# Batch-normalised matmul on one Trainium2 core: the first chunk of the last column tile in two halves

## The chip, the core and the metric

The kernel runs on one core of one Trainium2 chip. The metric is the device time of one execution in microseconds (us), lower is better. Four runs of the kernel before the change gave 218.57, 218.74, 219.96 and 220.45 us; their median is 219.35 us. One of them, the one of 218.57 us, was also profiled. The profiled execution has a span of 216.7 us from its first to its last instruction, so 1.87 us of its time lie outside the span.

## What is computed

```python
batch, m, k, n = 16, 512, 1024, 768

def reference(x, weight, gamma, beta, eps):
    y = np.matmul(x, weight)
    mean = np.mean(y, axis=(0, 1), keepdims=True)
    var = np.var(y, axis=(0, 1), keepdims=True)
    y_norm = (y - mean) / np.sqrt(var + eps)
    return (gamma * y_norm + beta).astype(np.float32)
```

All 8192 rows of `x` go through one 1024 x 768 matrix. Each of the 768 columns is then normalised with its own mean and variance over all 8192 rows. So no output of a column can be written before the last row of that column has been multiplied.

## The kernel before

**Tiling.** The 8192 rows are cut into C = 16 chunks of CH = 512, and each chunk into RT = 4 row tiles of 128. A chunk also has QPC = 2 halves of QR = 256 rows. The 768 columns are cut into NT = 6 tiles of 128. Column tiles 0, 1 and 2 go mostly by another way (rows on the partitions, with sums built up during the load); tiles 3, 4 and 5 are made with columns on the partitions: the 128 columns of the tile lie on 128 partitions and the 512 rows of a chunk lie along the free axis (`mm`, line 189). Statistics are then taken along the free axis with `bn` (line 311), and the product is kept in bf16 in SBUF with `keep` (line 342). The buffer that holds it is `y(nt, c)` (line 299), a slice of a tile that three chunks share.

**How a column tile is written out.** When all 16 chunks of a column tile have their statistics, VectorE (DVE) and ScalarE (ACT) work out one scale and one shift for each column: `finish` (line 361) for the last tile. Then each chunk goes through four steps, on four engines:

1. `norm` (line 375): DVE or ACT multiplies and adds, in place, on 128 x 512 bf16.
2. `turn_y` (line 387) lines up one transpose for each row tile; `turn_one` (line 396) issues it on TensorE (PE). Columns are on partitions and rows have to be there for the output, so each 128 x 128 block is transposed into PSUM (`o_ps`).
3. `out_copy` (line 400): ACT copies PSUM to an SBUF buffer and widens to float32.
4. `store` (line 415): SyncE (SP) issues the transfer to `out`. Each row of the output gets 128 floats, so the pieces written are 512 bytes long.

Column tiles 3 and 4 take chunks in pairs (512 KB for each store, from a buffer named `ring`). The last pair of column tile 4 is held back (`HELD = 1`) and issued by `held_outputs` (line 549) in the gap in which the last statistics are worked out. The last column tile, number 5, takes single chunks (256 KB for each store) in `last_outputs` (line 558). Its float32 buffers come from the pool of 11 buffers (`xtpool`, bufs = C - EARLY) that held the transposed input; they are called `o_sb`.

**What sets the order.** Nothing is issued where it is written. `at(t, fn, ...)` appends an event with a planned time; at the end all events are sorted by that time and called in turn. `seq` chains each instruction to the one before it on its engine, so the sorted list is the order of every engine. The planned times only set the order; at run time an engine runs its instructions in order and waits where an input or a buffer isn't ready. For the last chunk of the last column tile the matmul, its statistics and its copy are already split in two (`mm_half`, `bn_half`, `keep_half`, lines 325 to 340). Pools hand out buffers in turn: PSUM has 8 for the tag `b`, which the accumulators and the transposes share.

The order of the work at the end is therefore: on ACT the copy of the held pair (`ring`), the second `keep_half`, then 16 copies `o_sb`; on DVE `finish`, then 16 times `norm`; on PE the 8 transposes of the held pair, then 64 transposes; on SP the store of the held pair, then 16 stores.

Of the kernel before, what the change touches and what calls it, by code (L numbers as in the profile page):

```python
# [10 lines left out]
def kernel(  # L11
# [23 lines left out]
    nc = tc.nc  # L35
# [3 lines left out]
    ALU = mybir.AluOpType  # L39
# [9 lines left out]
    RT = CH // P  # L49
    C = M // CH  # L50
    QR = 256
    QPC = CH // QR
# [24 lines left out]
    def seq(bi):  # L77

        ins = bi.ins
        prev = last.get(ins.engine)  # L80
        if prev is not None:
            tc.add_manual_dep(
                ins, prev,
                mybir.DependencyInfo(mybir.DependencyClass.NoSync, mybir.DependencyReason.DATA),
                reason="order",
            )
        last[ins.engine] = ins.name
        return bi
# [6 lines left out]
    scale = singles.tile([P, NT], f32)  # L95
    shift = singles.tile([P, NT], f32)
# [202 lines left out]
    def y(nt, c):  # L299
        key, i = ((nt, c // GY), c % GY) if nt >= GA else ((0, c), nt)  # L300
        if key not in ygrp:
            y_sb = ypool.tile([P, GY, CH], bf16, tag="y")
            ygrp[key] = y_sb
        return ygrp[key][:, i]
# [70 lines left out]
    def norm(nt, c, eng):  # L375
# [5 lines left out]
        else:  # L381
# [2 lines left out]
                op0=ALU.mult, op1=ALU.add,  # L384
            ))

    def turn_y(nts, m0, tiles):

        o_ps = psum.tile([P, tiles, len(nts), P], bf16, tag="b")
        ops[nts, m0] = o_ps  # L390
        for s in range(tiles):
            c, i = divmod(m0 // P + s, RT)
            for a, nt in enumerate(nts):
                turns.append(((nts, m0), o_ps[:, s, a], y(nt, c)[:, i * P:(i + 1) * P]))
# [30 lines left out]
    def at(t, fn, *args):  # L425
        events.append((t, len(events), fn, args))
# [93 lines left out]
    for c in range(C):  # L520
        if c in COLS:
            for nt in range(GA):
                if c:
                    at(tk - 3.4 + 0.8 * nt, norm, nt, c, "act")
            for s in range(0, RT, 2):
                at(tk + 0.7 * s, turn_y, ga, c * CH + s * P, 2)
                at(tk + 0.7 * s + 1.9, out_copy, ga, c * CH + s * P, "act")
                at(tk + 0.7 * s + 2.7, store, ga, c * CH + s * P, 2)
            tk += 9.6 if c else 7.2
        else:  # L530
            for s in range(0, RT, 2):
                at(tr, norm_rows, c, s)
                at(tr + 1.1, shift_rows, c, s)
                at(tr + 3.0, store_rows, c, s)
                tr += 1.85

    def outputs(nt, t0, step):
        for b in range(C // 2):
            tb = t0 + step * b
            if nt == NT - 2 and b >= C // 2 - HELD:  # L540
                held.append(b)
                continue
            for i in range(2):
                at(tb - 2.2 + 0.5 * i, norm, nt, 2 * b + i, "act" if tb < tr + 2.0 and i == 0 else "dve")
            at(tb, turn_y, (nt,), 2 * b * CH, 2 * RT)
            at(tb + 2.2, out_copy, (nt,), 2 * b * CH, "act")
            at(tb + 2.3, store, (nt,), 2 * b * CH, 2 * RT)

    def held_outputs(nt, t0):

        for i, b in enumerate(held):
            for j in range(2):
                at(t0 - 3.0 + 0.4 * (2 * i + j), norm, nt, 2 * b + j, "dve")
            at(t0 + 0.05, turn_y, (nt,), 2 * b * CH, 2 * RT)
            at(t0 + 0.7 + 0.1 * i, out_copy, (nt,), 2 * b * CH, "act")
            at(t0 + 0.75 + 0.1 * i, store, (nt,), 2 * b * CH, 2 * RT)

    def last_outputs(nt, t0):

        for c in range(C):  # L560
            tb = t0 + 0.6 * c
            at(tb - 1.2, norm, nt, c, "dve")
            at(tb, turn_y, (nt,), c * CH, RT)
            at(tb + 0.5, out_copy, (nt,), c * CH, "act", True)
            at(tb + 0.6, store, (nt,), c * CH, RT)
# [3 lines left out]
    for nt in range(GA, NT):  # L569
        for c in range(EARLY, C):  # L570
            if (nt, c) == (NT - 1, C - 1):
                for q in range(QPC):
                    at(pe, mm_half, q)
                    pe += 0.9
                    at(pe + 0.2, bn_half, q)
                    at(pe + (0.4 if q == 0 else 1.0), keep_half, q)
                at(pe - 2.4, sum_up)
                continue
            for jws in halves:
                unit(nt, c, MM_US / 2 + (0.12 if nt == GA else 0.17), jws)  # L580
        if nt < NT - 1:
            at(pe + 0.55, finish_var, nt)
            at(pe + 1.6, finish_affine, nt)
        else:
            at(pe + 0.55, finish, nt)
        if nt == GA:
            outputs(nt, S + 37.0, 2.3)
        elif nt < NT - 1:
            outputs(nt, pe + 4.6, 1.85)
        else:  # L590
            held_outputs(nt - 1, pe)
            last_outputs(nt, pe + 3.0)
# [39 lines left out]
```

## Time and profile before

| what | us |
|---|---|
| median of four runs | 219.35 |
| lowest and highest run | 218.57, 220.45 |
| the profiled run | 218.57 |
| its span | 216.7 |
| PE busy (share of the span) | 200.3 (92%) |
| DVE busy | 155.8 (72%) |
| ACT busy | 120.8 (56%) |
| POOL busy | 134.2 (62%) |
| mean granted TensorE clock | 0.98 |

Over the whole span PE is the busiest engine. That share is an average, and the change touches only the last stage, from about 200 us on. In that stage these are the instructions of the last column tile (first and last start in us from the start of the span, and the duration of one):

| step | engine | how many | first start | last start | ns of one |
|---|---|---|---|---|---|
| `norm` | DVE | 16 | 200.16 | 205.02 | about 400 |
| transposes | PE | 64 | 200.63 | about 205.7 | about 220, one each 83 |
| `out_copy` to `o_sb` | ACT | 16 | 201.06 | 208.22 | 585 to 778 |
| issue of a store | SP | 16 | 201.67 | 211.23 | 372 to 637 |

Durations of neighbours overlap in the pipelines of the engines: DVE starts a `norm` every 0.32 us and ACT a copy every 0.48 us.

### The profile page before, as it was taken

What the parts mean: (1) busy time and instruction counts of PE and PEld (TensorE: products, weight loads), DVE (VectorE), ACT (ScalarE), POOL (GpSimd) and SP (SyncE); (2) the same over time, 40 slices, a digit from 0 to 9 for tenths busy, and PEclk for the clock granted to TensorE, in tenths of its full rate; (3) what the DMA queues carried; (4) which work ended last, traced back from release to release, by engine and by line L of the source; (5) the groups of instructions that cost most, each with busy time, mean ns of one, the idle gap of its engine ahead of it and who ended that gap; (6) DMA issues with size and microseconds to landing.
All of it is one profiled execution on the core that took longest, in us unless ns stands there. A gap on an engine that the chain in (4) does not pass through costs nothing.

```text
span 216.7 us, 3451 instructions
## 1 busy us (share of the span) xinstructions
PE 200.3 (92%) x1178; PEld 105.0 (48%) x1178; DVE 155.8 (72%) x263; ACT 120.8 (56%) x227; POOL 134.2 (62%) x153
## 2 busy tenths in 40 slices
PE   7998999999999999999999999999999979997900
PEld 2463545454544565645565544444444435554600
DVE  3223788896988789998654369978899999728900
ACT  2002463554553477646666415866866789976950
POOL 7888595978774799944558204999995963000000
PEclk9999999999999999999999999999999999999975
DMA  5999999999999999993000000897877989999998
GB/s 62 171 207 189 195 196 194 197 197 196 195 191 197 194 196 196 196 196 41 2 3 0 0 0 0 312 363 274 323 287 291 332 272 366 344 347 278 285 346 242
DMA packets 70161, 43.75 MB, mean 202 GB/s; under 512 B 4096, under 2 KB 69632, under 8 KB 70144
## 3 DMA queue, kind: packets, MB, share of 16 engines
q0 software_dynamic: 34624, 18.36, 61.8%
q1 hardware_dynamic: 35520, 25.18, 36.0%
q8 instruction: 9, 0.15, 0.3%
q14 instruction: 8, 0.07, 0.1%
HBM read 36.71 MB, written 25.17 MB: 285 GB/s over the span
## 4 chain that ended last, share of the span: by engine, by line
PE 75%; DVE 8%; DMA 5%; POOL 3%; issue 2%; ACT 2%; ACTq 1%; POOLq 0%
PE y_ps L196 39%; PE y_ps L186 29%; PE o_ps L398 5%; DMA w_sb<-in_weight_dram 2%; DMA ring<-in_x_dram 2%; DVE stats L316 2%; DVE y_sb L382 2%; DVE ring L283 2%; POOL w_sb L149 2%; DVE o_sb L283 1%; ACT o_sb L411 1%; POOL ring L162 1%; PE y_ps L330 1%; PE a_ps L272 1%; PE tot_ps L232 1%
## 5 line engine op out<-in xcount | busy, mean ns | idle before, releaser
L196 PE MATMUL y_ps<-xT_sb,w_sb 128*128 128x512 bf16 (+1 forms) x484 | 117.6, 381 | 0.7 <-DMA w_sb<-in_weight_dram 0.7
L196 PEld LDWEIGHTS <-w_sb 128*128 128x128 bf16 x484 | 46.0, 96 | 58.1 <-issue 1.6
L343 ACT CAST y_sb<-y_ps 128x512 bf16<-128x512 f32 x59 | 34.6, 587 | 52.7 <-DVE stats L316 49.8
L186 PE MATMUL y_ps<-w_sb,xT_sb 128*128 128x384 bf16 x384 | 63.4, 326 | 0.0
L162 POOL DMA_DIRECT2D ring<-in_x_dram x72 | 45.2, 633 | 12.2 <-DVE xT_sb L174 6.7
L316 DVE BATCH_NORM_STATS2 stats<-y_ps 128x6 f32<-128x512 f32 x58 | 39.1, 684 | 18.7 <-PE y_ps L196 18.7
L186 PEld LDWEIGHTS <-xT_sb 128*128 128x128 bf16 x384 | 37.6, 98 | 25.6
L174 DVE STREAM_TRANSPOSE xT_sb<-ring 128x1024 f32<-128x1024 f32 (+1 forms) x34 | 39.5, 1169 | 13.8 <-DMA ring<-in_x_dram 13.7
L212 POOL TENSOR_TENSOR sum<-sum,sq_sb 128x384 f32<-128x384 f32 x38 | 38.0, 1001 | 17.3 <-ACT sq_sb L208 15.7
L398 PE MATMUL o_ps<-ident,y_sb 128*128 128x128 bf16 x240 | 38.2, 219 | 3.6 <-DVE y_sb L382 2.5
L289 POOL TENSOR_TENSOR ring<-ring,sum 128x768 f32<-128x768 f32 x17 | 31.0, 1845 | 13.1 <-ACT sum L274 12.1
L215 DVE TENSOR_TENSOR sum<-y_ps,sum 128x384 f32<-128x384 f32 x48 | 26.1, 544 | 13.8 <-ACT sq_sb L208 12.7
L208 ACT ACTIVATE sq_sb<-y_ps 128x384 f32<-128x384 f32 x48 | 23.4, 493 | 13.9 <-PE y_ps L186 10.6
L221 ACT CAST y_sb<-y_ps 128x384 bf16<-128x384 f32 x48 | 22.9, 477 | 9.0 <-DVE sum L215 8.8
L411 ACT CAST ring<-o_ps 128x1024 f32<-128x1024 bf16 (+1 forms) x24 | 22.5, 955 | 4.3 <-PE o_ps L398 2.8
L398 PEld LDWEIGHTS <-y_sb 128*128 128x128 bf16 x240 | 19.4, 97 | 8.6 <-DVE y_sb L382 3.3
L382 DVE TENSOR_SCALAR y_sb<-y_sb,scale,shift 128x512 bf16<-128x512 bf16 x43 | 22.0, 562 | 0.0
L283 DVE TENSOR_TENSOR ring<-y_sb,a_ps 128x768 f32<-128x768 bf16 x17 | 15.8, 937 | 0.0
L289 POOL TENSOR_TENSOR o_sb<-o_sb,sum 128x768 f32<-128x768 f32 x7 | 13.1, 1868 | 2.9 <-DVE o_sb L283 2.9
L377 ACT ACTIVATE y_sb<-y_sb,shift,scale 128x512 bf16<-128x512 bf16 x17 | 13.5, 816 | 0.0
L155 PE MATMUL idle_ps<-idle_sb 128*128 128x512 bf16 x38 | 11.3, 466 | 1.2 <-DVE idle_sb L103 1.2
L411 ACT CAST o_sb<-o_ps 128x512 f32<-128x512 bf16 x16 | 7.9, 679 | 0.3 <-PE o_ps L398 0.3
(62 smaller groups left out, 50.1 us busy)
## 6 DMA issues: line engine op xcount, KB each, us to landing
ring<-in_x_dram POOLq DMA_DIRECT2D x56, 256.0 KB, 8.7
out_dram<-ring SPq DMA_DIRECT2D x25, 384.0 KB, 3.1
out_dram<-ring SPq DMA_DIRECT2D x16, 512.0 KB, 5.0
out_dram<-o_sb SPq DMA_DIRECT2D x16, 256.0 KB, 3.7
out_dram<-o_sb SPq DMA_DIRECT2D x7, 384.0 KB, 3.5
ring<-in_x_dram POOLq DMA_DIRECT2D x16, 128.0 KB, 5.1
w_sb<-in_weight_dram POOLq DMA_DIRECT2D x8, 96.0 KB, 4.5
w_sb<-in_weight_dram POOLq DMA_DIRECT2D x4, 192.0 KB, 5.0
```

The costliest lines, as they stand in the source:

```text
L162: seq(nc.gpsimd.dma_start(x_bf[32 * i:32 * i + 32], src[:, :, KQ * i:KQ * (i + 1)]))
L174: seq(nc.vector.transpose(dst[:, half, :, jw0:jw1], src[:, :, jw0:jw1]))
L186: seq(nc.tensor.matmul(y_ps, xT[c][:, jw, s * P:(s + 1) * P, e], w_sb[:, jw, e, 0:NA], start=(jw == 0 and e == 0), stop=(jw == JW - 1 and ...
L196: seq(nc.tensor.matmul(y_ps, w_sb[:, jw, e, nt * P:(nt + 1) * P], xT[c][:, jw, q0 * QR:q1 * QR, e], start=(jw == 0 and e == 0 and q0 == 0) ...
L212: seq(eng.tensor_add(acc, acc, py.pop(("sq", c, s))))
L215: seq(nc.vector.tensor_add(sum1, py["row", c, s][:, 0:NA], sum1))
L289: seq(nc.gpsimd.tensor_add(o_sb, o_sb, sum1[:, None, :].to_broadcast([P, 2, NA])))
L316: seq(nc.vector.bn_stats(stats_of(nt)[:, i, :], py[nt, c]))
L343: seq(nc.scalar.copy(y(nt, c), py.pop((nt, c))))
L382: seq((nc.vector if eng == "dve" else nc.gpsimd).tensor_scalar(y(nt, c), y(nt, c), scale[:, nt:nt + 1], shift[:, nt:nt + 1], op0=ALU.mult, ...
L398: seq(nc.tensor.transpose(dst, src, ident))
L411: seq(nc.scalar.copy(o_sb, src))
```

## The change

The first chunk (c = 0) of the last column tile is taken in two halves of 256 rows. Each half has its own `norm_half` on DVE (128 x 256 instead of 128 x 512), its own PSUM tile with two transposes, its own copy on ACT (128 x 256) into its own `o_sb`, and its own store (128 KB instead of 256 KB). Chunks 1 to 15 are as before.

```diff
+    def norm_half(nt, c, q):
+        part = y(nt, c)[:, q * QR:(q + 1) * QR]
+        seq(nc.vector.tensor_scalar(
+            part, part, scale[:, nt:nt + 1], shift[:, nt:nt + 1], op0=ALU.mult, op1=ALU.add))
+
     def turn_y(nts, m0, tiles):
...
         for c in range(C):
             tb = t0 + 0.6 * c
+            if c == 0:
+
+                for q in range(QPC):
+                    at(tb - 1.2, norm_half, nt, c, q)
+                    at(tb, turn_y, (nt,), q * QR, RT // QPC)
+                    at(tb + 0.4 + 0.1 * q, out_copy, (nt,), q * QR, "act", True)
+                    at(tb + 0.4 + 0.1 * q, store, (nt,), q * QR, RT // QPC)
+                continue
             at(tb - 1.2, norm, nt, c, "dve")
             at(tb, turn_y, (nt,), c * CH, RT)
             at(tb + 0.5, out_copy, (nt,), c * CH, "act", True)
```

In the compiled order of the engines this is one more instruction on DVE, on ACT and on SP, each at the place of the first chunk; the number and the order of the transposes on PE stay as they were, and so does everything ahead of this place.

## Prediction

> **What bounds the kernel now.** The page says PE 92% busy, but the change lies behind the last matmul, so I read the end alone. First the table of stages: busy time of each engine and, in the last two columns, the mean busy share of the DMA engines and what they moved.
>
> ```profile
> core 0: us, PE busy (x) PEld busy (x) DVE busy (x) ACT busy (x) POOL busy (x), PEclk, DMA share, GB/s
> 190.00:198.00 8.00, 8.00 (x57) 4.54 (x55) 4.29 (x10) 5.68 (x9) 0.00 (x0) 1.00 1.16 348
> 198.00:199.50 1.50, 0.97 (x13) 0.72 (x11) 0.93 (x4) 0.65 (x3) 0.00 (x0) 1.00 0.99 292
> 199.50:201.50 2.00, 0.87 (x12) 0.68 (x12) 1.79 (x8) 1.71 (x4) 0.00 (x0) 1.00 0.10 31
> 201.50:203.00 1.50, 1.50 (x22) 1.01 (x19) 1.50 (x6) 1.50 (x5) 0.00 (x0) 1.00 1.14 344
> 203.00:207.00 4.00, 2.87 (x36) 1.92 (x34) 2.41 (x8) 4.00 (x10) 0.00 (x0) 1.00 1.15 346
> 207.00:211.00 4.00, 0.00 (x0) 0.00 (x0) 0.00 (x0) 2.00 (x5) 0.00 (x0) 0.65 1.15 346
> 211.00:215.00 4.00, 0.00 (x0) 0.00 (x0) 0.00 (x0) 0.00 (x0) 0.00 (x0) 0.50 1.15 345
> 215.00:215.25 0.25, 0.00 (x0) 0.00 (x0) 0.00 (x0) 0.00 (x0) 0.00 (x0) 0.50 0.64 183
> 215.25:216.70 1.45, 0.00 (x0) 0.00 (x0) 0.00 (x0) 0.00 (x0) 0.00 (x0) 0.50 0.00 0
> ```
>
> There is one hole, 199.5 to 201.5, in which almost nothing is moved. From 201.5 to 215.1 the DMA engines move 344 to 346 GB/s without a break, although PE, DVE and ACT fall silent one after the other, ACT at 209.0. The last stage is a drain of fixed bytes at a fixed rate. It has the store of the held pair (512 KB) and 16 stores of 256 KB: 4.72 MB, at 346 GB/s 13.64 us; 201.5 + 13.64 = 215.14, which is where the traffic stops. Behind it 1.56 us remain to the end of the span, and 1.87 us outside it.
>
> So the question is what starts the drain. The timeline of SP's issues:
>
> ```profile
> 200.53 0.37 SPq L416 DMA_DIRECT2D out_dram<-ring  x1
> 201.67 0.37 SPq L416 DMA_DIRECT2D out_dram<-o_sb  x1
> 202.16 0.50 SPq L416 DMA_DIRECT2D out_dram<-o_sb  x1
> 211.23 0.64 SPq L416 DMA_DIRECT2D out_dram<-o_sb  x1
> ```
>
> The first line is the held pair, the second chunk 0 (the one that is split), the third chunk 1, the last chunk 15. The DMA view of 199.5 to 201.5, in 40 slices of 0.05 us, shows where the bytes of the held pair begin:
>
> ```profile
> GB/s 41 41 41 61 41 41 41 41 41 41 41 61 41 41 41 41 41 41 41 61 41 31 20 20 20 20 0 0 0 0 0 0 0 0 0 0 0 0 31 174
> ```
>
> They begin in the last two slices, at 201.43: 0.9 us after their issue. At 346 GB/s 512 KB last 1.52 us, to about 202.97. Chunk 0 is issued at 201.67; with the same 0.9 us its bytes are there at 202.57, **0.40 us before the DMA engines need them**. The drain is started by the held pair, not by chunk 0, and chunk 0 is early already.
>
> The chain of waits names something else, and it is a trap here:
>
> ```profile
> 200.16 0.42 DVE y_sb L382
> 200.58 0.05 issue
> 200.63 3.96 PE o_ps L398 x48
> 204.59 0.03 ACTq L411
> ...
> 208.51 0.49 ACT o_sb L411
> ```
>
> It runs through the `norm` of chunk 0 and the transposes and ends at ACT's last copy at 209.0. It is a chain of instructions and has no transfer in it; the 6.1 us of pure DMA behind it are not on it.
>
> **The change, part by part.** Durations are from this one execution; the row for the copies and the one for a half:
>
> ```profile
> L411 ACT CAST o_sb<-o_ps 128x512 f32<-128x512 bf16 x16 | 7.9, 679 | 0.3 <-PE o_ps L398 0.3
> L340 ACT CAST y_sb<-y_ps 128x256 bf16<-128x256 f32 x2 | 0.7, 372 | 0.0
> ```
>
> *DVE: one `norm` becomes two.* There is no row of this operation at 256 columns. One of 512 takes 0.41 us and the next starts after 0.32. A half can't need less than half of that spacing, 0.16, nor more than the whole, 0.32; its duration lies between 0.21 and 0.41. I take 0.20 and 0.25, near the lower end, as the statistics instruction falls from 0.69 to 0.43 with half the columns. The first half is done at 200.41 instead of 200.57, the second at 200.61; chunks 1 to 15 come 0.08 us later (bounds 0 to 0.32). DVE finishes at 205.4, while ACT takes a chunk only every 0.48 us and gets later and later behind it: cover enough, even for 0.32.
>
> *PE.* The same 64 transposes, in the same order, with one more wait, of the third transpose on the second half. Behind that wait all later transposes are queued, and ACT waits for them. Before, PE began 0.06 us after `norm` and ACT began 0.43 us after PE (200.63 to 201.06). Two fewer transposes at 0.083 make that 0.26 us. First half: 200.41 + 0.06 + 0.26 = 200.73. Second half 0.20 later, 200.93.
>
> *ACT: one copy becomes two.* The second `keep_half` stands ahead and holds ACT until 200.77. So the first copy starts at 200.77 rather than 201.06, lasts 0.37 by the row above, and ends at 201.14 instead of 201.64: 0.50 us earlier. The second ends about 0.3 later, at 201.44. One more instruction costs ACT about 0.1 us, but it starts 0.29 earlier, so the copy of chunk 1 is not later than before (201.54).
>
> *SP: one issue becomes two.* Free of the held pair at 200.90, SP issues the first half at about 201.17 and the second at 201.6 (the issue is 0.37, and 0.49 lie between 201.67 and 202.16). Chunk 1 then goes at 202.1 to 202.2, against 202.16. From there SP is its own bound: an issue every 0.62 to 0.69 us, with the copies ahead of it. Chunk 15 stays at 211.2, at worst one issue (0.69) later, 211.9. Its bytes could start at 212.1 or 212.8; the DMA engines come to it at 215.14 - 0.76 = 214.38. Cover 1.6 us or more.
>
> *The cover at the start.* Bytes of the first half ready at 202.07, needed at 202.97; of the second ready at 202.5, needed at 203.35; of chunk 1 ready at 203.1, needed at 203.73. The stream has no hole before and none after. The 0.5 us won on chunk 0 lengthens a queue that is waiting already. It is worth **nothing**. Only if the held pair's store were not in front would it be worth its 0.50.
>
> *Buffers and semaphores.* 17 `o_sb` tiles instead of 16 go round 11 buffers. Copies of chunks 11 to 15 wait for the same stores as before (the two halves stand for chunk 0, so chunk 15 still waits for chunk 4). New is only a wait of chunk 10's copy (start about 205.84) for the first half's store, whose bytes are through at 203.35. In the compiled order each store waits for the store eight before it: chunk 7's issue (205.87) now waits for the first half, also done. PSUM's 8 buffers shift by one; the transposes of chunk 7 (about 203) wait for the first half's copy, done at 201.14. None of these comes near.
>
> *DMA engines: 16 stores become 17, the bytes stay.* Here there is no cover: what a transfer costs beyond its bytes goes straight onto the end. The pieces stay 512 bytes long. The rows: 512 KB stores run at 348 GB/s (190 to 198), 256 KB stores at 346 (203 to 211). Two of 256 KB take 2 x 0.758 = 1.515 us, one of 512 KB 1.507: about 0.01 us for each further transfer. The Trainium skill, "DMA: Bandwidth & Descriptors", says otherwise: its "Anatomy of one DMA" gives a fixed cost of about 2.0 us for each DMA (fitted on GpSimd's path, while these go through SP), and its rules for kernel authors say to use 1 MiB or more and to coalesce small transfers, which speaks against a split. By the rule, if it were paid in series, the sum would be +2.0 us; but then 16 stores of 0.76 us could not stand one behind the other at 346 GB/s. It is latency, hidden by queueing: the 0.9 us between issue and bytes is part of it, and the next store's bytes run meanwhile. I take 0.02, with bounds 0 and 2.0.
>
> **Sum.** Removed from the path 0, added 0.02: 218.59 us against the profiled 218.57. That execution was the quickest of four, 0.78 below the median, so against the median: 219.35 + 0.02 = 219.4 us.
>
> **Rivals.**
>
> 1. *The chain of waits is right and the end follows chunk 0.* For: DVE, PE, ACT and SP do run one from the other from 200.16 on. Against: 6.1 us of traffic behind the chain, and 0.40 us of the held pair's bytes still to go when chunk 0's come. Price: all 0.50 us, 219.35 - 0.50 = 218.85. This too is within 1%.
> 2. *The smaller transfers cost DMA time (slower).* Place: between the bytes of the two halves and chunk 1, 202.97 to 203.8. Price: one to two times the fixed cost where queueing doesn't hide it. It shows at once, as the DMA engines have no slack; a hole of 1.0 us makes 220.35, one of 2.0 makes 221.35, and from 2.2 us on it would be more than 1%. For: 128 KB stores don't occur in the trace of before. Against: the 0.01 us between 512 KB and 256 KB, and a queue that already holds over 0.4 us of work.
> 3. *The change doesn't do what it says.* ACT is busy to 200.77 with `keep_half`; if the half copy also took as long as the whole (0.58), the first store would go 0.3 earlier and chunk 1 about 0.3 later. With 0.6 us of cover for chunk 1 the time is again 219.4.
>
> **How the numbers follow.** Forecast (no hole, no gain) 0.83, rival 3 with the same time 0.05, rival 1 0.05, rival 2 0.07. A median of this kernel can't be told from no change within 1% (four runs lie 0.9% apart), 2.2 us. Chances: faster by over 1% 0.03 (no case reaches it; left for a mechanism that I don't see), slower by over 1% 0.05 (the far end of rival 2 and the same reserve), within 1% 0.92. The range has to hold the scatter of the runs, 218.57 to 220.45; rival 1 moves its lower end down a little, rival 2 its upper end up: 218.3 to 220.6.
>
> **What would show it.** In the changed trace: the first `o_sb` store is issued near 201.2, the second near 201.6; the held pair's store still at 200.5; the DMA engines still start at about 201.4 and run at 345 GB/s without a hole; traffic stops at 215.1 to 215.2. A step is wrong if the stream starts earlier than the held pair's store plus 0.9 us, if a slice between 202 and 204 falls below 340 GB/s, or if chunk 15's bytes are late, a drop just ahead of 215. I am wrong altogether if the traffic stops by more than 0.3 us from 215.1 with the held pair's store where it was.

## The result: no change that can be told, and the profile after

| | before | after |
|---|---|---|
| median, us (runs) | 219.70 (64) | 219.66 (43) |
| lowest to highest, us | 218.38 to 221.93 | 218.37 to 220.42 |
| span of the profiled execution, us | 216.7 | 218.3 |

The ratio of after to before is 0.9997, with a 95% interval of 0.9985 to 1.0009. In the ratios, here and below, slow runs (over 1.5% above the fastest of the same kernel) are left out.

The number alone says little. The forecast of 219.4 us stood on a median of four runs, 219.35; with 64 runs that median is 219.70. No change, a gain of 0.5 us and a loss of 1 us would all have fallen into the forecast's range of 218.3 to 220.6. The narrower interval of the ratio leaves out the 0.50 us of rival 1 (0.9977) and the hole of 1.0 us of rival 2 (1.0046). What decides is the trace.

The two profiled executions differ by 1.6 us, and the wrong conclusion lies close at hand: that the change cost 1.6 us. The chain of waits at the start shows where they come from. First the kernel before, then the changed one (start, duration, what):

```profile
12.92 5.38 DMA w_sb<-in_weight_dram
18.29 0.14 issue
18.43 5.58 PE y_ps L196 x24
```

```profile
13.28 6.62 DMA w_sb<-in_weight_dram
19.90 0.14 issue
20.03 5.58 PE y_ps L196 x24
```

The load of the weights began 0.36 us later in the changed kernel and took 6.62 us instead of 5.38, and the main matmuls began at 20.03 instead of 18.43. This is 180 us ahead of the first changed instruction, and it differs from execution to execution: over the fourteen profiles of this study (the same code up to this place) the same row starts between 18.09 and 20.51 us. That alone is a scatter of 2.4 us; the runs of the kernel before scatter by 3.55 us in all, those of the changed one by 2.05. So nothing in the tail can be read from span against span. From here on every time of the tail is given from the start of the last statistics' aggregation on DVE, written A; these rows of the timeline fix it, before and after:

```profile
199.03 0.25 DVE L364 BATCH_NORM_AGGREGATE mv<-fin 128x2 f32<-128x21 f32 x1
```

```profile
200.63 0.25 DVE L364 BATCH_NORM_AGGREGATE mv<-fin 128x2 f32<-128x21 f32 x1
```

The stages of the changed kernel, moved by the same 1.6 us (last two columns: mean busy share of the DMA engines, GB/s):

```profile
201.11:203.11 2.00, 0.90 (x9) 0.49 (x10) 1.79 (x8) 1.89 (x5) 0.00 (x0) 1.00 0.11 35
203.11:204.61 1.50, 1.50 (x20) 1.11 (x20) 1.50 (x6) 1.46 (x4) 0.00 (x0) 0.89 1.14 344
204.61:208.61 4.00, 3.74 (x40) 3.56 (x37) 2.60 (x9) 4.00 (x10) 0.00 (x0) 0.61 1.15 345
212.61:216.61 4.00, 0.00 (x0) 0.00 (x0) 0.00 (x0) 0.00 (x0) 0.00 (x0) 0.50 1.15 345
216.61:216.86 0.25, 0.00 (x0) 0.00 (x0) 0.00 (x0) 0.00 (x0) 0.00 (x0) 0.50 0.66 191
```

The same hole, the same 345 GB/s behind it, the same end. In slices of 0.05 us, from A + 2.5 to A + 4.5, the changed kernel shows no hole where the bytes of the held pair, of the two halves and of the first part of chunk 1 follow each other:

```profile
GB/s 307 348 338 338 338 348 358 369 348 348 338 338 338 348 358 369 348 348 338 338 338 348 358 369 348 348 338 338 338 328 338 338 358 369 348 348 318 338 338 338
```

SP's issues in the changed kernel:

```profile
202.14 0.37 SPq L421 DMA_DIRECT2D out_dram<-ring  x1
202.89 0.37 SPq L421 DMA_DIRECT2D out_dram<-o_sb  x1
203.35 0.48 SPq L421 DMA_DIRECT2D out_dram<-o_sb  x1
203.93 0.46 SPq L421 DMA_DIRECT2D out_dram<-o_sb  x1
212.86 0.60 SPq L421 DMA_DIRECT2D out_dram<-o_sb  x1
```

The held pair is issued at A + 1.51 (before 1.50), the first half at A + 2.26 (chunk 0 before: 2.64), the second at 2.72, chunk 1 at 3.30 (before 3.13), chunk 15 at 12.23 (before 12.20). The store did get away 0.38 us sooner; nobody was waiting for it. The end of the traffic, in slices of 0.04 us, of the kernel before from 214.3 us on and of the changed one from 215.9 us on:

```profile
GB/s 333 320 346 346 346 346 371 307 358 371 320 346 371 333 358 346 371 307 358 308 167 103 39 0 0 0 0 0 0 0 0 0 0 0 0 0 0 0 0 0
```

```profile
GB/s 358 346 308 359 346 307 384 346 320 371 371 320 333 384 346 307 384 346 320 358 231 116 39 13 0 0 0 0 0 0 0 0 0 0 0 0 0 0 0 0
```

Both fall in the 21st slice, 215.1 and 216.7: A + 16.1 in both. This distance, A to the end of the traffic, is the measure of all experiments below. It is read in slices of 0.02 us, as the end of the last one that moves more than 173 GB/s, half of the full rate. Two profiles of one kernel (the held pair in two, below) came out 0.02 us apart, so differences of 0.03 us and less are not read as such. The interval of the ratio above is 0.5 us wide.

### The profile page after: what moved, and what is told of

Read it like the earlier page. It is cut to its first block, busy times and chain, and to the rows that moved or that the text cites. A ratio compares the mean times of both kernels' runs of the same rounds, so it can differ in the third digit from the quotient of the medians.

```text
span 218.3 us, 3456 instructions
## 1 busy us (share of the span) xinstructions
PE 201.3 (92%) x1178; PEld 106.4 (49%) x1178; DVE 156.0 (71%) x264; ACT 121.3 (56%) x228; POOL 134.2 (61%) x153
## 4 chain that ended last, share of the span: by engine, by line
PE 73%; DVE 8%; DMA 5%; ACT 4%; POOL 3%; issue 2%; ACTq 1%; POOLq 0%
PE y_ps L196 39%; PE y_ps L186 29%; PE o_ps L403 3%; DMA w_sb<-in_weight_dram 3%; ACT o_sb L416 3%; DMA ring<-in_x_dram 2%; DVE stats L316 2%; DVE ring L283 2%; DVE y_sb L382 2%; POOL w_sb L149 2%; DVE o_sb L283 1%; POOL ring L162 1%; PE y_ps L330 1%; PE a_ps L272 1%; PE tot_ps L232 1%
## 5 line engine op out<-in xcount | busy, mean ns | idle before, releaser
L403 PE MATMUL o_ps<-ident,y_sb 128*128 128x128 bf16 x240 | 39.1, 231 | 3.6 <-DVE y_sb L389 1.6
L403 PEld LDWEIGHTS <-y_sb 128*128 128x128 bf16 x240 | 21.0, 103 | 7.9 <-ACT y_sb L377 2.3
L416 ACT CAST o_sb<-o_ps 128x512 f32<-128x512 bf16 (+1 forms) x17 | 8.1, 637 | 0.2
```

The lines of the kernel that those rows point to most:

```text
L403: seq(nc.tensor.transpose(dst, src, ident))
L416: seq(nc.scalar.copy(o_sb, src))
```

## Experiments

Each row is one profile; each ratio is to runs of the kernel before that were taken beside it.

| run | first `o_sb` store issued, A + | traffic ends, A + | ratio to before, 95% interval |
|---|---|---|---|
| before | 2.64 | 16.09 | |
| after | 2.26 | 16.11 | 0.9997 [0.9985, 1.0009] |
| one instruction late | 3.31 | 16.40 | one run |
| three late | 3.99 | 17.08 | 1.0047 [1.0026, 1.0068] |
| three late, halves | 3.71 | 17.11 | 1.0062 [1.0033, 1.0090] |
| four chunks in halves | 2.26 | 16.71 | 1.0046 [1.0019, 1.0073] |
| all chunks in halves | 2.26 | 20.29 | 1.0196 [1.0148, 1.0245] |
| no held pair | 2.65 | 15.73 | 1.0032 [1.0010, 1.0055] |
| no held pair, halves | 2.25 | 15.70 | 1.0003 [0.9974, 1.0033] |
| no held pair, filled | 2.65 | 15.74 | one run |
| no held pair, halves, filled | 2.26 | 15.67 | one run |
| held pair in two | 2.65 | 15.73 | 0.9987 [0.9968, 1.0006] |
| held pair in two, again | 2.65 | 15.75 | 0.9999 [0.9979, 1.0019] |
| held pair in two, halves | 2.26 | 15.72 | 0.9976 [0.9958, 0.9994] |

In the four slower kernels with a ratio (three late, three late with halves, four and all chunks in halves) what the trace adds, 0.99, 1.02, 0.62 and 4.20 us or 0.45, 0.46, 0.28 and 1.9%, lies inside the interval of the ratio. "All chunks in halves" has only four runs.

### How long is the cover? Chunk 0 made late

Nothing but a delay is added to the kernel before, one or three instructions ahead of chunk 0's `norm`:

```diff
+            if c == 0:
+                at(tb - 1.3, spend, nt, LATE)
             at(tb - 1.2, norm, nt, c, "dve")
...
+    def spend(nt, count):
+        junk = sqpool.tile([P, CH], bf16, tag="sq")
+        for _ in range(count):
+            seq(nc.vector.tensor_scalar(
+                junk, y(nt, 0), scale[:, nt:nt + 1], shift[:, nt:nt + 1],
+                op0=ALU.mult, op1=ALU.add))
```

> The kernel before, with one extra DVE instruction (a norm-like 128x512 bf16 operation into a scratch buffer, about 0.32 us) put ahead of the norm of chunk 0 of the last column tile; nothing else. It makes chunk 0 and all behind it 0.32 us late. Measure: from the start of the last bn_aggr on DVE to the end of the DMA traffic, 16.1 us before (199.03 to 215.1). Theory (the held pair's store covers chunk 0 by 0.40 us): no hole in the traffic, 16.1 us again. Rival (the end follows chunk 0, as the chain of waits says): 16.4 us.

> The kernel before with three such extra instructions, 0.97 us. Theory: 0.40 us of it are covered, a hole of 0.57 us opens between the held pair's bytes and chunk 0's, the measure goes from 16.1 to 16.7 us, the time up by 0.6 us (0.3%). Rival (the end follows chunk 0): 17.1 us, up by 1.0 us. If the drain had more cover than I think: 16.1.

The delays came out larger than planned: whatever followed one of these instructions, another of them or chunk 0's `norm`, started 0.45 us behind it, not 0.32 (why is not shown), and in the first run TensorE's clock was low as well (last section). What counts is how late the store is issued: 3.31 - 2.64 = 0.67 us in the one, 3.99 - 2.64 = 1.35 in the other. The DMA view of the two runs, A + 3 to A + 5 in slices of 0.05 us:

```profile
GB/s 338 328 348 358 348 358 348 358 338 328 348 358 348 358 348 358 338 328 277 174 41 0 0 0 72 184 317 338 358 358 338 338 338 348 369 338 358 358 338 328
```

```profile
GB/s 338 358 369 348 338 348 348 338 338 358 369 348 338 348 348 338 338 358 257 134 41 0 0 0 0 0 0 0 0 0 0 0 0 0 0 0 0 0 143 236
```

The held pair's bytes run out at about A + 3.95 in both, and then the engines stand idle until chunk 0's arrive. The ends are late by 16.40 - 16.09 = 0.31 and 17.08 - 16.09 = 0.99 us. So 0.67 - 0.31 = 0.36 us and 1.35 - 0.99 = 0.36 us were free. The forecast had 0.40. In the first run no hole was expected, as the planned delay of 0.32 us was less than the cover; 0.67 us was more. That the end follows chunk 0 from the start would have given 0.67 and 1.35; it is refuted. The cover is shown, and its size.

### With the cover gone, do the halves pay?

The same three instructions in the changed kernel:

> The changed kernel (chunk 0 in halves) with the same three extra instructions ahead of its first half. With the cover gone the halves should pay. Theory: the first half's store is issued about 0.4 us sooner than chunk 0's in the run with three and no halves, so the hole is about 0.2 us instead of 0.57, the measure about 16.3 us and the time about 0.4 us (0.2%) under that run's. If a second hole opens behind the first half (128 KB last only 0.38 us, the second half is issued 0.46 later), up to 0.1 us more. Rival (smaller transfers cost DMA time): as late as without halves or later, 16.7 us or more.

17.11 against 17.08 us: no gain. The first half did go 0.28 us sooner (3.71 against 3.99), but the second at 4.18 and chunk 1 at 4.72, where the run without halves had chunk 1 at 4.48. The holes in the traffic behind the held pair were 0.68, 0.15 and 0.18 us, 1.0 in all; without halves there was one of 0.98. The 0.4 us that I had expected were wrong. But TensorE's clock behind the gap was 0.50 here and 1.00 there, so the comparison wasn't clean. The next ones have no held pair at all, before and changed:

```diff
-    HELD = 1
+    HELD = 0
```

> The kernel before without a held pair (the last pair of column tile 4 goes out in its turn, under the matmuls), so that chunk 0's store starts the drain. Theory: 8 transposes more between the matmuls, about 0.45 us, so the last statistics come 0.45 us later; the drain starts 0.9 us after chunk 0's issue and has 4.19 MB instead of 4.72: the measure falls from 16.1 to about 15.7 us. Together 0.0 us, within 0.2%. Here the DMA engines are idle for about 1 us longer and nothing covers chunk 0.

> The changed kernel without a held pair: chunk 0 in halves with no cover ahead. Theory: the first half is issued 0.4 us sooner than chunk 0 in the run without a held pair and without halves, and the drain starts that much sooner, minus at most 0.1 us for a hole between the two halves: measure about 15.3 to 15.4 us, time 0.3 to 0.4 us (0.15 to 0.2%) under that run's. Rival (halves are worth nothing or less in themselves): the same measure as that run, about 15.7.

The measure without halves was as expected (15.73, expected 15.7); the time was 0.1 to 0.55% up where no change was expected. Of that the trace accounts for little: from the first main matmul to A it is 181.06 us instead of 180.60, 0.46 more, and the tail is 0.36 less. Nor is the size firm: the medians of all runs, 220.11 and 219.71, stand 0.18% apart where the ratio says 0.32%. The rest stays open. The measure with halves, 15.70, missed the 15.3 to 15.4: the gain was 0.03. Again the clock was low, in the run with halves alone at the decisive place. So both were run once more with TensorE kept busy in its gap:

```diff
             held_outputs(nt - 1, pe)
+            at(pe + 0.06, fill, 7)
...
+    def fill(count):
+        f_ps = psum.tile([P, CH], f32, tag="b")
+        for _ in range(count):
+            seq(nc.tensor.matmul(f_ps, w_sb[:, 0, 0, 0:P], w_sb[:, 0, 0, 0:CH], start=True, stop=True))
```

> The run without a held pair and without halves, with seven matmuls of 128x512 on weights into a PSUM tile that nobody reads, put in TensorE's gap while the last statistics are worked out. They keep the granted clock at 1.00, which fell to 0.50 behind that gap in the runs without a held pair, at different moments. Measure: start of the last bn_aggr on DVE to the end of the traffic, 15.73 us without the filling. Theory: chunk 0's transposes ran at full clock there already, so 15.7 us again; the clock is 1.00 until the transposes are through. Rival (the filling itself delays the first transposes): more than 15.8.

> The same filling in the run without a held pair and with chunk 0 in halves, which took 15.70 us with a clock of 0.50 from the first transposes on. This asks what halves are worth with no cover and at full clock. Theory (SP's spacing of 0.46 to 0.57 us for each issue is wider than the 0.38 us that a half's bytes last): first half issued at 2.26, second at 2.72, chunk 1 at 3.3 us behind the start of the last bn_aggr; holes of about 0.1 and 0.2 us between their bytes; the measure is 15.5 to 15.6 us, 0.15 us under the run without halves and not 0.4. Rival A (the 0.40 us of my forecast's first rival come in full): 15.3 us. Rival B (halves give everything back at full clock too): 15.7 us.

The clock was 1.00 in both until the transposes were through. SP's issues, without halves (A at 200.86) and with them (A at 201.45):

```profile
203.51 0.37 SPq L421 DMA_DIRECT2D out_dram<-o_sb  x1
203.99 0.44 SPq L421 DMA_DIRECT2D out_dram<-o_sb  x1
```

```profile
203.71 0.37 SPq L426 DMA_DIRECT2D out_dram<-o_sb  x1
204.18 0.42 SPq L426 DMA_DIRECT2D out_dram<-o_sb  x1
204.69 0.45 SPq L426 DMA_DIRECT2D out_dram<-o_sb  x1
```

And the traffic of the run with halves, A + 3 to A + 5:

```profile
GB/s 0 0 0 143 225 328 348 379 348 338 287 154 62 31 174 287 358 338 348 338 328 277 113 41 10 143 276 328 348 358 328 358 328 369 338 348 348 369 328 348
```

Three blocks can be seen: the first half, the second, then chunk 1 and all that follows. Between them are dips that cost 0.16 and 0.18 us of full traffic. A half's bytes last 0.38 us (128 KB at 346 GB/s), but SP's issues stand 0.47 and 0.51 us apart, and each block begins 0.9 to 1.0 us behind its issue, so the DMA engines wait for SP twice. Without halves chunk 0's bytes last 0.76 us and cover SP's 0.48 to chunk 1. The first bytes come 0.40 us sooner with halves; the two dips take 0.34 of that back, which leaves 0.06. The ends agree: 15.67 against 15.74. So the halves are worth about **0.07 us** with no cover and at full clock, not 0.38. Neither the 0.15 us that I had expected nor a full loss was right. Each of the two ends comes from one profile, so the 0.07 us are not much more than the view can tell; that most of the 0.40 is given back is shown.

### More halves: what a further store costs

Chunks 0 to 3, then all chunks, in halves (`c * CH + q * QR` in place of `q * QR`):

```diff
-            if c == 0:
+            if c < 4:
```

> The changed kernel with chunks 0 to 3 of the last column tile in halves: 20 stores at the end instead of 17 (16 before). Theory: a further transfer costs the DMA engines about 0.01 us, and SP's three further issues (about 0.5 us each) still fit into its lead of 2.2 us: the measure is 16.1 to 16.3 us, the time within 0.1% of before. Rival (each further transfer costs part of a fixed 2.0 us of DMA time): at 0.5 us each 18.1 us, at 2.0 us each 24 us.

> The changed kernel with all 16 chunks of the last column tile in halves: 32 stores of 128 KB. The same bytes. Measure: start of the last bn_aggr on DVE to the end of the traffic, 16.1 us before. Theory: DMA engines don't mind (32 stores cost some 0.2 us), but SP must issue 32 times at 0.46 to 0.62 us: its last issue at 201.28 + 31 x 0.46 to 0.62 = 215.5 to 220.5, the bytes end some 1.3 us later, so SP becomes the bound and the time goes up by 2 to 7 us; the traffic then has holes, and the gaps between issues show no waiting for ACT. Rival (fixed cost of each transfer in the DMA engines): also up, but the DMA engines' share stays at its full value to the end without holes while GB/s falls.

Four chunks ended at 16.71, 0.62 us late, where I had expected 0.2 at most (the rival's 2.0 us are the figure that the prediction cites). The holes (0.08, 0.16, 0.15 and 0.18 us) open from A + 5.85 on: the bytes of the sixth half, issued at A + 4.95. From the second half on each costs SP 0.53 to 0.58 us and gives the DMA engines bytes for 0.38, so it eats nearly 0.2 us of what is queued, and what was queued was half a microsecond. The 2.2 us of lead that I had counted on build up only later, with whole chunks. In the run with all chunks in halves this goes on to the end. Here are two neighbouring issues and the stage view, then the traffic from 209 to 213 us in slices of 0.1:

```profile
209.90 0.44 SPq L421 DMA_DIRECT2D out_dram<-o_sb  x1
210.44 0.44 SPq L421 DMA_DIRECT2D out_dram<-o_sb  x1
```

```profile
202.60:205.60 3.00, 3.00 (x26) 1.56 (x24) 3.00 (x13) 3.00 (x12) 0.00 (x0) 0.52 1.15 344
206.00:220.00 14.00, 4.29 (x32) 2.17 (x30) 3.55 (x14) 6.68 (x19) 0.00 (x0) 0.62 0.82 245
```

```profile
GB/s 348 154 56 266 358 343 256 41 195 333 343 333 103 82 271 328 343 185 113 246 317 338 297 77 149 323 358 343 144 97 292 343 348 241 51 230 358 338 318 82
```

There is one issue each 0.54 us, and 128 KB / 0.54 us = 243 GB/s, close to the 245 of the stage. Between the stores the traffic falls to between an eighth and a third, and in each it reaches the full rate again. SP keeps this spacing even where ACT pauses (0.99 us ahead of its copy at 212.16, for a buffer whose store had not landed). Nor does it wait for ACT: the view of waits names ACT in front of SP's issues, but from the ninth half on each copy had ended 2.1 to 3.6 us before its store was issued. The store eight before is no bound either: it lands at most 2.7 us after its issue, and eight issues take 4.3 us. So SP's issuing is the bound here, not a cost of small transfers in the DMA engines; with such a cost they would be busy all the time, and their share fell from 1.15 to 0.82. What the 0.44 us of one issue consist of is not shown.

### Where a split does pay: the held pair

The held pair's store starts the drain, so it was split instead of chunk 0:

```diff
-            at(t0 + 0.05, turn_y, (nt,), 2 * b * CH, 2 * RT)
-            at(t0 + 0.7 + 0.1 * i, out_copy, (nt,), 2 * b * CH, "act")
-            at(t0 + 0.75 + 0.1 * i, store, (nt,), 2 * b * CH, 2 * RT)
+            for j, tj in enumerate((0.7, 0.72)):
+                at(t0 + 0.05, turn_y, (nt,), (2 * b + j) * CH, RT)
+                at(t0 + tj, out_copy, (nt,), (2 * b + j) * CH, "act")
+                at(t0 + tj + 0.01, store, (nt,), (2 * b + j) * CH, RT)
```

> The kernel before with the held pair, not chunk 0, in two (each of its two chunks with its own PSUM tile, copy and 256 KB store; the copies stay behind the last square root on ACT). Theory: the held pair's store starts the drain, so this is where a split pays: the first copy ends at about 200.1 instead of 200.50, the drain starts 0.4 us sooner and ends 0.4 us sooner; chunk 0 (bytes at about 202.6 to 202.7) then comes 0.1 to 0.2 us after the pair's bytes are through, which gives that much back: measure 15.8 to 15.9 us, time down by 0.2 to 0.3 us (0.1%). Rival (the end follows chunk 0): 16.1 or, as ACT has one more instruction ahead of chunk 0's copy, 16.2.

> The run with the held pair in two once more, for a narrower interval: measure 15.75 us as before, 0.37 us under the kernel before; time down by 0.2 to 0.4 us, a ratio of 0.998 to 0.999.

> The held pair in two and chunk 0 in halves as well. With the held pair in two the cover of chunk 0 is used up (a hole of 0.05 us). Theory: the halves close that hole and can't give more, as the drain is then whole from its start at 2.05 us behind the start of the last bn_aggr: measure 15.70 us, 0.05 under the run with the held pair in two; in the time not to be told from it. Rival (halves worth 0.4 us once uncovered): 15.35, which the 13.64 us of bytes behind 2.05 leave no room for. If chunk 1 comes late behind the two issues: 15.8.

The first store of the held pair in two (A at 200.45), and the traffic from A + 1.95 to A + 3.95 in slices of 0.05 us:

```profile
201.52 0.37 SPq L416 DMA_DIRECT2D out_dram<-ring  x1
```

```profile
GB/s 51 164 287 328 338 348 348 379 338 358 338 338 338 348 348 338 318 379 338 358 338 338 338 348 348 379 338 358 338 338 328 205 236 246 317 369 338 369 328 348
```

The first store went at A + 1.07 instead of 1.50, the traffic began at A + 2.0 instead of 2.45 and ended at 15.73, 0.36 us sooner; the second time it ended at 15.75. A dip at A + 3.5, worth 0.05 us, was left between the pair's bytes and chunk 0's: the cover was just used up. Here a piece is 256 KB, whose 0.76 us are longer than SP's spacing between two issues (0.48 us), and between the two pieces there is no dip. With chunk 0 in halves as well the dip at A + 3.5 was gone and one of 0.02 us stood at A + 4.25; the measure was 15.72. By the dips the halves are worth some 0.03 us once the held pair starts sooner; by the ends it is not to be told from nothing.

The traces say 0.34 to 0.37 us sooner, 0.16%. That lies inside all three intervals, but only the last one (0.9958 to 0.9994) leaves out no change. The times fit a gain of 0.16% in all three; a difference among them is not shown, and neither is it shown from the times alone that the first two are faster.

## Why the prediction was right, point by point

**The bound.** Right, and shown: the last stage is a drain of fixed bytes. It begins 0.9 us after the held pair's issue and ends 13.6 us later, in both kernels. The cover of 0.40 us was measured twice as 0.36.

**DVE.** A half has a spacing of 0.26 us and lasts 0.34 to 0.35, where I took 0.20 and 0.25, near the lower bound. Chunk 1's `norm` came 0.19 us later (A + 1.65 against 1.46), not 0.08. It was hidden, as forecast: ACT's copy of chunk 1 was 0.04 us later for it.

**PE and ACT.** The first half's copy began at A + 1.86; forecast 1.74. It waited for the transposes and not, as I had it, for `keep_half`. It lasts 0.37, as the row for a half said, and with that rival 3 is out: the change does what it says. Chunk 1's copy began at A + 2.55 against 2.51 before: nearly level.

**SP.** The issues stood at 2.26, 2.72, 3.30 and 12.23; the forecast was 2.14, 2.6, 3.1 to 3.2 and 12.2 to 12.9. Chunk 1's bytes had 0.5 us left instead of the 0.63 forecast. The step held, with 0.13 us less to spare than forecast.

**DMA engines.** One more transfer: 16.09 and 16.11, so the 0.02 us is not contradicted and lies below what the view can show. The fixed 2.0 us of the rule that I weighed doesn't occur in series: in the run with 32 stores the full rate comes back with each. That the 0.9 us between issue and bytes is part of these 2.0, as the forecast has it, no run shows. The forecast's sign of a wrong step, a slice below 340 GB/s, was set too tight: slices of 328 and 338 stand in the trace of the kernel before too, with no hole there.

**Rival 1 was mis-sized.** It was right to give it little; but its price, and the sentence "Only if the held pair's store were not in front would it be worth its 0.50", took the gain on the first bytes for the gain on the end. I had overlooked what must follow behind the first half in time to keep the engines busy. Without the held pair the halves were worth about 0.07 us.

**Rival 2** named the right place, the stretch from the halves to chunk 1, and the wrong cause. What thins the traffic there is the time that SP needs for each issue, not the DMA engines. With one chunk in halves the half microsecond queued ahead absorbs it; with four chunks it does not.

## What to carry to other kernels

When the end of a kernel is a drain at a constant rate, look for the transfer that starts the drain. To speed up a piece that queues behind it is worth nothing as long as its bytes are ready before those in front are through. Splitting a piece so that its first part leaves sooner gains at most what the second part and the next piece can follow up: if the bytes of a part last less long than issuing it (here 0.38 against about 0.5 us), most of the gain is given back, and the rest of the queue is thinned. And a change in the tail is best read from a mark close to it, not from span to span: here the start of the kernel alone scattered by 2.4 us.

## What the runs showed of the hardware that I had not expected

**TensorE's clock fell at the gap, at different moments.** While the last statistics are worked out TensorE is idle for 1.6 to 2.1 us, with three late instructions for 3.0. In the kernel before the granted clock stayed at 1.00 through the transposes; in the changed one it was 0.50 from about A + 3.7 to A + 7.1; in the run with one late instruction it was already 0.55 in the half microsecond of the first transposes, and ACT's first copy came 1.11 us after `norm` began instead of 0.90. Without a held pair and with halves, unfilled (A at 201.55) and filled (A at 201.45), the stages next to the first transposes:

```profile
203.55:204.55 1.00, 1.00 (x11) 0.89 (x10) 1.00 (x5) 0.78 (x3) 0.00 (x0) 0.50 0.13 38
```

```profile
203.45:204.45 1.00, 0.96 (x14) 0.68 (x12) 1.00 (x5) 0.95 (x3) 0.00 (x0) 1.00 0.12 37
```

The column ahead of the DMA share is the granted clock; at half clock TensorE gets through 11 transposes instead of 14 in that microsecond. In nine of the twelve profiles with nothing filled in, the clock fell between A + 1.9 and A + 4.7, and it stayed at 0.50 for 3.4 us, in one of them for 6.8. A gap of 1.6 us was followed by the fall in some and not in others (before: no; after: yes). The Trainium skill, "TensorE: Matmul & The Clock Gate", Part 1, has the clock fall after an idle window of about 3.4 us that runs freely. That the moment differs from one execution to the next, and the 3.4 us at half clock, agree with it; but here no gap is longer than 3.0 us, and the clock fell behind gaps of 1.6 too. In the changed kernel ACT, and not TensorE, was the slower of the two by then, so it cost nothing; in the run with one late instruction it cost those 0.2 us, a term that the forecast did not have.

**An issue on SP took longer when transfers were queued**: 0.37 us for the first, 0.44 to 0.45 in the run where SP was the bound, and in the kernel before and the changed one 0.46 to 0.64 with the DMA engines saturated. With the time between two issues that is one store each 0.46 to 0.7 us in these two. The size hardly counted: in the run with four chunks in halves the halves behind the first took 0.44 to 0.48 us each, and the two whole chunks that followed 0.44 and 0.48.
